# Three small loads ahead of the first one, tiles moved by 64 bytes, and the matmuls around two transposes split one and three, in a fused matmul, GELU, matmul

## The chip, the cores and the metric

The kernel runs on one core of one Trainium2 chip. The metric is device time in microseconds (us) of one execution. Five executions of the kernel before took 120.43, 120.38, 120.18, 120.31 and 118.75 us, with a median of 120.31. A profile is one execution recorded by the hardware profiler, and it names the engines PE (matrix engine, with its weight loads as PEld), DVE (vector), ACT (scalar), POOL (GpSimd) and SP (which only issues transfers here).

## What is computed

```python
h = a @ b                                  # a 1024x1024, b 1024x2048, float32
h = 0.5*h*(1 + tanh(sqrt(2/pi)*(h + 0.044715*h**3)))
out = h @ c                                # c 2048x1024
```

The tanh form of GELU is one ACT function. The kernel works with bf16 operands and with sums and differences of them in a 32-bit format.

## The kernel before

**The whole.** The first product is computed transposed, 128 of its 2048 columns at a time, for two halves (0 and 1) of 512 rows of `a`. GELU writes the result to `hT[h]`, which the second product uses as its stationary operand. The first 4 column tiles are made by plain matmuls (`block`, `mm1`). The other 12 and the second product go through `seven`, a scheme that forms the four blocks of a 2x2 block product from seven block products (`zero`, `one` and `two`). There DVE and ACT make the sums (`Seven.dve`, `plain_s`, `plain_t`) and PE accumulates in PSUM.

**The order is written by hand.** Every engine executes its instructions in the order in which the function states them. Waits between engines follow from the tiles that the instructions share.

**Loads.** SP issues twelve loads of 512 KB: eight of `a` into the two `sta` tiles (`load_a(h, q)`: half h, a quarter q of the columns, in runs of 1024 bytes), and four of the first 512 columns of `b` into `stb` (`load_b`, in runs of 2048 bytes). The last load of `a` releases a one-column copy on POOL (`gate`, L82), and behind it POOL issues the other loads of `b` and those of `c`, with a cast to bf16 on the way (L87 to L93). ACT issues no load. Its first instruction is a GELU on one column (L83), ahead of which its function table is loaded.

**The opening.** PE first multiplies zeros (`stir`, four pieces on `warm`) while the first load is under way. `cast_a` then casts a quarter of `a` to bf16 (`ab`), on DVE, on ACT or half on each. `turn(h, q, i, ab)` transposes it in two steps, n = 0 and n = 1, of four PE transposes each. Both steps write the same PSUM tile `pt`, and after each of them DVE copies 128x512 elements from it to `aT` (L131). `next(tn)` runs one step. Between the two steps of a turn stand some matmuls of the step before. For the turns of half 1 these are the last two tiles of a `block` of four (the first two stand ahead of the turn). For half 0 they are a block of three.

```python
block(0, range(2), (3,))
tn = turn(1, 1, 7, ab)
next(tn)
block(0, range(2, 4), (3,))
next(tn)
```

The opening is followed by `seven(zero)`, `seven(one)` and `seven(two)`, nearly all of whose PE work is L195.

**Tiles.** `consts` is a pool of small tiles. The pools `keep`, `big` and `small` come behind it in memory, so its length moves every other tile. The first of them, `c_sb`, starts at byte 17,856 of its partition, which is 34 times 512 plus 448. All later tiles have lengths that are multiples of 512, and so have the same remainder. The tag `o` is a ring of four tiles of 128x512 for results (`plus`, and the copies in `done2`), from which the stores are made.

**Stores.** `done2(i, l, j, p)` stores a block of 128x512 of the result through SP. Blocks with (i, l) = (0, 0) are stored in two halves of 256 columns. The last two pieces of the kernel are made from a ring of their own (`e`, L377 to L379).

Of the kernel before, what the change touches and what calls it, by code (L numbers as in the profile page):

```python
# [9 lines left out]
F32 = mybir.dt.float32  # L10
# [9 lines left out]
def kernel(ctx, tc, a, b, c, out):  # L20
    nc = tc.nc
# [3 lines left out]
    H = 512  # L25
# [8 lines left out]
    consts = ctx.enter_context(tc.tile_pool(name="consts", bufs=1))  # L34
# [11 lines left out]
    def pieces(tag, bufs, shape, dt, name):  # L46
        return small.tile(shape, dt, name=name, tag=tag, bufs=bufs)
# [5 lines left out]
    gate = consts.tile([128, 1], F32, name="gate")  # L53
    g = consts.tile([128, 1], F32, name="g")

    c_sb = keep.tile([128, NT, P], BF16, name="c_sb")
    hT = [keep.tile([128, NT, H], BF16, name=f"hT{h}") for h in range(2)]
    aT = slot("a", [128, 2, KT, H], BF16, "aT")
# [8 lines left out]
    def load_a(h, q):  # L67
        nc.sync.dma_start(out=sta[q // 2][:, h, q % 2],
                          in_=av[:, 4 * h:4 * h + 4, ds(q * 256, 256)])

    def load_b(q):
        nc.sync.dma_start(out=stb[:, 2 * q:2 * q + 2], in_=bv[:, 2 * q:2 * q + 2, 0:H])

    load_a(0, 0)
    load_b(0)
    load_a(1, 0)
    for q in range(1, 4):
        load_a(0, q)
        load_b(q)
        load_a(1, q)  # L80
# [7 lines left out]
    for n in range(2):  # L88
        for k in range(0, KT, 4):
            nc.gpsimd.dma_start(out=b2[:, k:k + 4, ts(n, H)],  # L90
                                in_=bv[:, k:k + 4, ds(1024 + n * H, H)])
# [9 lines left out]
    def mm1(p, t, h, ks):  # L101
        for k in ks:
            nc.tensor.matmul(p, b1[:, k, ts(t, 128)], aT[:, h, k],  # L103
                             start=(k == 0), stop=(k == KT - 1))
# [20 lines left out]
    def turn(h, q, i, ab):  # L125

        pt = bank(i, (128, 2, H), BF16, "pt")
        for n in range(2):
            for m in range(4):
                nc.tensor.transpose(pt[:, n, ts(m, 128)], ab[:, m, ts(n, 128)], ident)  # L130
            nc.vector.tensor_copy(aT[:, h, 2 * q + n], pt[:, n])  # L131
            yield
# [6 lines left out]
    def block(h, tiles, ks):  # L139
        for k in ks:  # L140
            for t in tiles:
                mm1(ps[h, t], t, h, (k,))
# [93 lines left out]
    cast_b(3)  # L236
    ab = cast_a(1, 1, nc.vector, nc.scalar)
    block(0, range(4), (2,))
    block(0, range(2), (3,))
    tn = turn(1, 1, 7, ab)  # L240
    next(tn)
    block(0, range(2, 4), (3,))
    next(tn)
    zero.t1(4, 1)
    ab = cast_a(0, 2, nc.scalar, nc.scalar)
# [6 lines left out]
    cast_b(5)  # L252
    ab = cast_a(1, 2, nc.vector, nc.scalar)
    block(0, range(4), (4,))
    block(0, range(2), (5,))
    tn = turn(1, 2, 7, ab)
    next(tn)
    block(0, range(2, 4), (5,))
    next(tn)
    zero.t1(4, 2)  # L260
    ab = cast_a(0, 3, nc.scalar, nc.scalar)
# [169 lines left out]
    def store(mt, q0, w, ot, eng=None):  # L431
        (eng or nc.sync).dma_start(out=out[ts(mt, 128), ds(q0, w)], in_=ot)

    def done2(i, l, j, p):
        if (i, l) == (1, 0):
            ot = pieces("o", 4, [128, H], F32, "ot")
            nc.vector.tensor_copy(ot, p)
            p = ot
        n = 2 if (i, l) == (0, 0) else 1
        for q in range(n):  # L440
            r = ds(q * (H // n), H // n)
            store(4 * i + j, l * H + q * (H // n), H // n, p[:, r])

    def between2(n):
        if n == "P1":
# [11 lines left out]
        elif n == "P73":  # L457
            two.t4(two.t[1], 4)

    seven(two, done2, between2)  # L460


# [28 lines left out]
```

## Time and profile before

| What | Value |
|---|---|
| Median of five executions | 120.31 us (118.75 to 120.43) |
| The profiled execution: its own time | 120.43 us |
| Its span, first to last instruction | 118.7 us |
| PE busy | 113.4 us, 96% of the span |
| DVE, ACT, POOL busy | 90.5, 59.3 and 11.0 us |
| First load, from its issue until what waits for it can go on | 0.74 to 4.28 us |
| Opening (turns and plain matmuls) on PE | 5.05 to about 27.2 us |
| The three `seven` stages on PE | about 27.2 to 115.4 us |
| SP's loads | 512 KB each, 9 us in the middle from issue to landing |

The profiled time is 1.7 us above the span; this lies around the program's instructions. A busy PE means that some matmul is in the pipeline. Whether it runs at its full rate is seen only from how far the starts of two matmuls lie apart.

### The profile page before, as it was taken

Reading aid. Unit: us, or ns where it says so; the run is one execution under the profiler, and the core shown is the slowest. Engines: PE = TensorE matmul, PEld = TensorE weight load, DVE = VectorE, ACT = ScalarE, POOL = GpSimd, SP = SyncE. Lnnn points to the kernel's source line nnn. Section 1 sums busy time; section 2 is a strip of 40 time slices with the busy share of each in tenths; the row PEclk is TensorE's granted clock in tenths of the full one; section 3 lists DMA queues with packets and bytes.
Section 4 is the critical chain, followed back from the end, with each engine's and each line's share of the span. In section 5 each row is a group of like instructions: output and inputs, shape, how many; then the busy total and the mean of one; then the engine's idle time right before and its main releaser. Section 6 shows DMA issues by size and latency. Waiting matters only on the chain.

```text
span 118.7 us, 1478 instructions
## 1 busy us (share of the span) xinstructions
PE 113.4 (96%) x540; PEld 77.8 (66%) x540; DVE 90.5 (76%) x107; ACT 59.3 (50%) x99; POOL 11.0 (9%) x21
## 2 busy tenths in 40 slices
PE   5899999999999999999999999999999999999990
PEld 5464554554777545888887444488888888888860
DVE  0331666889999799971779999999999986964570
ACT  5066577489648989446769446900042992000000
POOL 2000029722332000000000000000000000000000
PEclk9999999999999999999999999999999999999999
DMA  2999999999999999997000000061000002004993
GB/s 87 281 372 364 365 355 336 207 207 206 206 208 211 211 211 213 212 210 147 3 0 0 0 6 0 0 200 65 0 0 0 0 0 94 0 29 175 363 355 139
DMA packets 13542, 17.91 MB, mean 151 GB/s; under 512 B 736, under 2 KB 8928, under 8 KB 13536
## 3 DMA queue, kind: packets, MB, share of 16 engines
q0 software_dynamic: 5344, 7.34, 34.8%
q1 hardware_dynamic: 8192, 10.49, 26.0%
q8 instruction: 4, 0.07, 0.2%
q14 instruction: 2, 0.02, 0.0%
HBM read 20.97 MB, written 4.19 MB: 212 GB/s over the span
## 4 chain that ended last, share of the span: by engine, by line
PE 91%; DMA 3%; DVE 2%; issue 0%
PE ps L195 74%; PE ps L103 12%; PE pt L130 4%; DMA sta<-in_a_dram 3%; DVE aT L131 1%; PE ps L114 1%; DVE ab L99 1%; DVE ot L378 0%
## 5 line engine op out<-in xcount | busy, mean ns | idle before, releaser
L195 PE MATMUL ps<-x,s 128*128 128x512 f32 x128 | 29.6, 391 | 0.0
L195 PEld LDWEIGHTS ps<-x,s 128*128 128x128 f32 x128 | 24.0, 188 | 5.1
L195 PE MATMUL ps<-x,x 128*128 128x512 f32 x96 | 22.9, 394 | 0.0
L195 PEld LDWEIGHTS ps<-x,x 128*128 128x128 f32 x96 | 18.0, 188 | 3.9
L103 PE MATMUL ps<-aT,b 128*128 128x512 bf16 x64 | 17.5, 402 | 0.0
L301 ACT ACTIVATE v<-ps 128x512 f32<-128x512 f32 x10 | 6.0, 598 | 19.4 <-PE ps L195 19.4
L195 PE MATMUL ps<-c_sb,hT 128*128 128x512 bf16 (+1 forms) x72 | 14.2, 356 | 0.0
L195 PE MATMUL ps<-x 128*128 128x512 f32 x56 | 13.2, 393 | 0.0
L131 DVE COPY aT<-pt 128x512 bf16<-128x512 bf16 x16 | 6.8, 423 | 8.2 <-PE pt L130 8.2
L195 PEld LDWEIGHTS ps<-x 128*128 128x128 f32 x56 | 10.2, 188 | 2.7 <-ACT u L301 0.4
L195 PEld LDWEIGHTS <-hT 128*128 128x128 bf16 x72 | 6.9, 98 | 7.0 <-issue 0.5
L107 ACT ACTIVATE hT<-ot 128x512 bf16<-128x512 f32 x18 | 10.6, 627 | 1.6 <-DVE ot L306 1.4
L306 DVE TENSOR_TENSOR ot<-ps,u 128x512 f32<-128x512 f32 x10 | 6.8, 690 | 5.4 <-ACT u L301 5.4
L306 DVE TENSOR_TENSOR ot<-ps,v 128x512 f32<-128x512 f32 x10 | 6.7, 688 | 5.3 <-DMA out_dram<-ot 3.9
L195 PE MATMUL ps<-aT,b 128*128 128x512 bf16 x48 | 10.7, 379 | 0.0
L153 DVE TENSOR_TENSOR x<-c_sb 128x1024 fp32r<-128x1024 bf16 x8 | 9.2, 1217 | 0.0
L130 PEld LDWEIGHTS <-ab 128*128 128x128 bf16 x64 | 5.0, 102 | 6.3 <-issue 3.4
L103 PEld LDWEIGHTS <-b 128*128 128x128 bf16 x64 | 6.0, 103 | 4.7 <-issue 1.1
L195 PEld LDWEIGHTS <-b 128*128 128x128 bf16 x48 | 4.6, 98 | 5.7 <-issue 0.3
L107 ACT ACTIVATE hT<-ps 128x512 bf16<-128x512 f32 x14 | 7.3, 597 | 1.6 <-PE ps L103 1.6
L97 ACT ACTIVATE ab<-sta 128x512 bf16<-128x512 f32 x10 | 6.0, 625 | 4.2 <-DMA sta<-in_a_dram 3.4
L301 ACT ACTIVATE u<-ps 128x512 f32<-128x512 f32 x10 | 5.9, 597 | 3.4 <-PE ps L195 3.2
(39 smaller groups left out, 116.2 us busy)
## 6 DMA issues: line engine op xcount, KB each, us to landing
sta<-in_a_dram SPq DMA_DIRECT2D x8, 512.0 KB, 9.1
c_sb<-in_c_dram POOLq DMA_DIRECT2D x8, 512.0 KB, 19.8
b<-in_b_dram POOLq DMA_DIRECT2D x6, 512.0 KB, 11.8
out_dram<-ot SPq DMA_DIRECT2D x12, 256.0 KB, 2.1
stb<-in_b_dram SPq DMA_DIRECT2D x4, 512.0 KB, 8.7
out_dram<-ot SPq DMA_DIRECT2D x8, 128.0 KB, 2.0
```

The source lines that it names most:

```text
L97: nc.scalar.activation(dst, src, AF.Copy)
L99: nc.vector.tensor_copy(dst, src)
L103: nc.tensor.matmul(p, b1[:, k, ts(t, 128)], aT[:, h, k], start=(k == 0), stop=(k == KT - 1))
L107: nc.scalar.activation(hT[h][:, t], p, AF.Gelu_apprx_tanh)
L114: nc.tensor.matmul(ps[0, 3][:, 0:w], warm[:, 0:128], warm[:, 0:w], start=True, stop=True, skip_group_check=True)
L130: nc.tensor.transpose(pt[:, n, ts(m, 128)], ab[:, m, ts(n, 128)], ident)
L131: nc.vector.tensor_copy(aT[:, h, 2 * q + n], pt[:, n])
L153: nc.vector.tensor_tensor(out=dst[:, r], in0=x[:, r], in1=y[:, r], op=op)
L195: nc.tensor.matmul(p[:, ds(c0, w)], l[:, k, ts(j, 128)], r[:, k, ds(c0, w)], start=(start and k == 0), stop=(k == self.kt - 1), skip_group ...
L301: nc.scalar.activation(st, p, AF.Copy)
L306: nc.vector.tensor_tensor(out=ot, in0=p, in1=st, op=ADD)
```

## The change

Four things are changed.

1. `consts` gets one more tile of 64 bytes for each partition, `room`, that nothing uses. All tiles of the pools behind it move by 64 bytes, `c_sb` to 17,920, which is 35 times 512.
2. Ahead of SP's loads three small loads are issued from ACT: 12, 8 and 4 rows of `b`, 2048 bytes each, to as many partitions (from 96, 64 and 32 on) of a tile `lag`, which nothing reads. The loads are spread over 12, 8 and 4 of the 16 DMA engines. `lag` is the first tile taken from the ring `o`, so all later ones move on by one place.
3. In turns (1, 1) and (1, 2) one matmul of the block stands ahead of the turn and three between its two steps, in place of two and two.
4. `done2` stores the blocks with (i, l) = (0, 0) whole, as all others: three stores of 256 KB in place of six of 128 KB.

```diff
     g = consts.tile([128, 1], F32, name="g")
 
+    consts.tile([128, 16], F32, name="room")
+
     c_sb = keep.tile([128, NT, P], BF16, name="c_sb")
...
+    lag = pieces("o", 4, [128, H], F32, "lag")
+    for n in (12, 8, 4):
+        nc.scalar.dma_start(out=lag[8 * n:9 * n], in_=b[0:n, 0:H])
 
     load_a(0, 0)
...
     block(0, range(4), (2,))
-    block(0, range(2), (3,))
+    block(0, range(1), (3,))
     tn = turn(1, 1, 7, ab)
     next(tn)
-    block(0, range(2, 4), (3,))
+    block(0, range(1, 4), (3,))
     next(tn)
...
-    block(0, range(2), (5,))
+    block(0, range(1), (5,))
     tn = turn(1, 2, 7, ab)
     next(tn)
-    block(0, range(2, 4), (5,))
+    block(0, range(1, 4), (5,))
     next(tn)
...
-        n = 2 if (i, l) == (0, 0) else 1
-        for q in range(n):
-            r = ds(q * (H // n), H // n)
-            store(4 * i + j, l * H + q * (H // n), H // n, p[:, r])
+        store(4 * i + j, l * H, H, p)
```

## The prediction

> **What bounds the kernel now.** I read the page first, for which engine sets the end:
>
> ```profile
> span 118.7 us, 1478 instructions
> ...
> PE 113.4 (96%) x540; PEld 77.8 (66%) x540; DVE 90.5 (76%) x107; ACT 59.3 (50%) x99; POOL 11.0 (9%) x21
> ...
> PE 91%; DMA 3%; DVE 2%; issue 0%
> ```
>
> PE carries the chain that ended last; transfers are in it for 3% (the first load), DVE for 2%. From 27.4 to 115.4 us the chain is one piece, L195, 400 matmuls in 88.0 us. At the 0.216 us that lie between two starts of 512 columns in the trace, and half of it for the 16 short ones, these need 84.7 us. Nothing of the change touches this stretch but the place of its operands. What can be won lies ahead of it, so I read the chain in order of time (start, length, what):
>
> ```profile
> 0.74 3.54 DMA sta<-in_a_dram
> ...
> 8.15 2.52 PE ps L103 x6
> ...
> 13.62 1.29 PE ps L103 x6
> 14.91 0.24 PE pt L130 x4
> 15.15 0.02 issue
> 15.18 0.44 DVE aT L131
> 15.61 0.04 issue
> 15.65 0.38 PE pt L130 x4
> 16.04 0.65 PE ps L103 x3
> 16.68 0.25 PE pt L130 x4
> 16.94 0.65 PE ps L103 x3
> 17.59 0.29 PE pt L130 x4
> ```
>
> Three things are to be seen. The first load starts everything. The first six plain matmuls take 0.42 us each and later ones 0.215: PE ran at half its clock until 10.49 us, where the trace's only record of a granted full clock begins (the page's clock row shows full speed in the first slices only because no record covers them). And in turn (1, 1) the chain leaves PE for DVE's copy between the two steps (15.15 to 15.65), while in turn (0, 2), with three matmuls between its steps, it stays on PE.
>
> Last, the timeline, for what the first step of a turn waits for (start, length, engine, line, idle time before and its releaser):
>
> ```profile
> 14.00 0.42 DVE L99 CAST ab<-sta 128x512 bf16<-128x512 f32 x1
> ...
> 18.25 0.70 DVE L99 CAST ab<-sta 128x512 bf16<-128x512 f32 x1
> ...
> 19.01 0.23 PEld L130 LDWEIGHTS <-ab 128*128 128x128 bf16 x4 [0.34 <-DVE ab L99]
> ```
>
> The casts of turns (1, 1) and (1, 2) are the same work; the second takes 0.70 us, while POOL is issuing its loads (17.08 to 23.0 us), and PE's weight loads wait for it.
>
> **One and three.** The starts of PE's matmuls give the hole: in turn (1, 1) the second matmul between the steps starts at 15.191 and the first transpose of step 1 at 15.654, 0.463 us later where 0.216 is due: 0.247 lost. In turn (0, 2), with three between, it is 0.248, so 0.032 lost. A third matmul fills the hole: 0.247 - 0.032 = 0.215 us, one matmul. It is won only if step 0 can start one matmul earlier. In turn (1, 1) DVE's cast ends at 14.42, a weight load follows such an end by 0.06 (18.95 to 19.01), so step 0 can start at 14.48; with five matmuls instead of six behind the transposes of turn (0, 1) it is due at 14.54. It fits by 0.06 us: 0.215 won. In turn (1, 2) the cast ends at 18.95, and step 0 starts at 19.01 already, 0.01 late. One matmul earlier it would be due at 18.79 and would stall 0.22 us for the cast: the hole moves from behind step 0 to ahead of it, and nothing is won. That the cast shrinks to 0.42 (then 0.215 more) needs it to miss POOL's issuing. POOL's gate opens when the last load of `a` has landed (16.93), and the cast stays inside the 6 us of issuing even if that is 1.7 us sooner. Bounds 0 and 0.215; I take 0, by the row of this very cast. What is late next is the copy's end again, by 0.03 us.
>
> **64 bytes.** The packets of SP's loads last 46 ns for 1024 bytes and 84 to 88 ns for 2048 (the trace's packets; middle values). [...] The first load is 512 packets, 32 for each DMA engine: 32 x 4 ns = 0.13 us sooner (bounds 0 and 0.26).
>
> Over the whole of SP's loads (1.8 to 20.7 us, about 350 GB/s) 8% is 1.5 us, but this is hidden: the transposes of turn (0, 3) start at 20.83 and ACT's cast for them ends at 19.63, over 1 us earlier, and no PE wait in this profile is for a load behind the first. Should PE come earlier by more than that, the loads would bind. The last store, 128 runs of 1024 bytes, 8 for each DMA engine, gains 8 x 4 ns = 0.03 us on the tail.
>
> **Three small loads.** ACT has no DMA issue in this profile, so the cost is bounded. On ACT: SP's issues take 0.33 us (128 packets) to 0.42 (512), so three take 1.0 to 1.3 us. They push the table load (0.73 to 2.01) and the column behind it (2.03) to an end near 3.6 us; ACT's next work is at 6.64, after an idle of 4.41. Hidden with 3 us to spare. On the DMA engines: 3, 2, 1 and 0 packets of 84 ns on four engines each, 0.25 us at most, if they go ahead of the first load. [...] No trace here shows an ACT queue. If issuing too is shared, SP's first issue could stand behind one small issue, 0.33 us, or all three, 1.0. Below nothing: the small loads could take the slow first packets (200 to 280 ns on some engines near 2.1 us) off the first load, up to 0.2 us. So the first load lands between 0.2 sooner and 1.25 later; I take 0.25 later, by the packet row, and with the 0.13 above 0.1 later.
>
> This delay does not cost its full length: if the clock is released at 10.49 whatever PE's start, a shift of 0.1 us moves 0.1 us of half-rate work behind the release, where it takes half. Cost 0.05 us (bounds -0.2 and +0.5).
>
> **Ring and stores.** The ring `o` only changes the numbers of its tiles. Three issues fewer on SP at 77 to 80 us; no PE wait is for them, and SP idles 17.7 us behind. Where they matter is the release of an `o` tile for DVE 15 us later. 0.
>
> **The sum.** -0.215 + 0.05 - 0.03 = -0.2 us of the profiled 120.43, which is 120.2. The profiled execution stands 0.12 above the median; from 120.31 the same step gives 120.1. That is 0.2%, well within the 1% that a measurement of this kernel can tell from no change.
>
> **The rivals.** *The clock decides (chance 0.27).* The fifth execution, 118.75, is 1.7 us below the profiled one. [...] Then PE meets the loads, the 8% count too, 0.2 to 0.5 us: 118.75 - 0.2 - 0.3 = 118.3, between 118.0 and 118.6. [...]
>
> *A window later (0.08), the slower side.* [...]
>
> *No effect of the two turns (within the forecast's chance).* The cast of turn (1, 1) runs into POOL's issues too, if the gate opens before 14.0; 120.3.
>
> **How the numbers follow.** Forecast 0.65: between 119.7 (both turns, no delay) and 120.7 (no turn, 0.5 of delay). Early clock 0.27, late clock 0.08. The range from 118.1 to 120.9 leaves out the late clock and a tail on either side. Faster by over 1% (below 119.1): 0.27; slower by over 1% (above 121.5): 0.08; within: 0.65.
>
> **What would show it.** In the profile of the changed kernel the chain stays on PE through turn (1, 1), with 0.25 us ahead of its second step; turn (1, 2) keeps a hole of 0.2 us ahead of its first step, behind a cast of 0.70. Packets of 1024 bytes take 42 ns (46 would say that 64 bytes are nothing), and POOL's gate opens 1 us or more before 16.93. The first cast starts at about 4.4 instead of 4.30, and the first plain matmuls lie 0.43 apart until 10.5. What makes me wrong is the release of the clock at another window, or a first load later by 1 us.

## The result, and the profile after

| | before | changed |
|---|---|---|
| median of all executions | 119.01 us (76) | 118.30 us (39) |
| lowest, highest | 118.60, 120.76 | 118.09, 120.41 |
| executions below 119.65: number, median | 50, 118.94 | 25, 118.24 |
| executions above it: number, median | 26, 120.37 | 14, 120.13 |
| the profiled execution: its own time, span | 120.43, 118.7 | 120.17, 118.4 |

The ratio is 0.9921, with a 95% interval of 0.9901 to 0.9941. It leaves out executions more than 1.5% above the fastest of their kernel, which is all 14 of the changed kernel's upper group but only a part of before's, so that I also compare like with like: 118.24 against 118.94 is 0.994, and 120.13 against 120.37 is 0.998. The changed kernel is faster by 0.7 us where both are in the lower group and by 0.2 where both are in the upper one, less than 1%.

Both kernels have two groups of executions, and here nothing between them. The traces tell which is which: in profiles of the lower group TensorE's full clock is granted between 4.2 and 6.8 us after the start of the span, in those of the upper group between 9.97 and 10.60. I call them early and late clock. (Until then matmuls start 0.43 us apart instead of 0.215.) Four of the five times that the forecast started from were late; of 76 only 26 are. The changed kernel has the same share of late ones beside it, 36% against 34%. The share itself wanders: in the groups of runs below, 31 to 55% of the executions of the kernel before are late.

The profiled execution of the changed kernel is a late one too, as that of before is, and so the two can be compared line by line. The page of the changed kernel:

```profile
span 118.4 us, 1478 instructions
...
PE 112.7 (95%) x540; PEld 77.7 (66%) x540; DVE 90.5 (76%) x107; ACT 59.2 (50%) x99; POOL 11.5 (10%) x21
...
PE 91%; DMA 3%; DVE 2%; issue 1%
```

PE is busy for 0.7 us less, and the chain has the same shares. The chain of waits that ended last in the changed kernel, in order of time (start, length, what):

```profile
0.74 4.10 DMA sta<-in_a_dram
...
8.71 1.98 PE ps L110 x6
...
13.64 1.08 PE ps L110 x5
14.72 0.22 PE pt L137 x4
14.95 0.65 PE ps L110 x3
15.60 0.25 PE pt L137 x4
...
18.06 0.71 DVE ab L106
18.77 0.05 issue
18.82 0.40 PE pt L137 x4
19.21 0.65 PE ps L110 x3
...
27.19 87.99 PE ps L202 x400
```

The first load takes 4.10 us in place of 3.54. In turn (1, 1) (14.72 to 15.85) the chain now stays on PE, with five matmuls ahead and three between the steps. In turn (1, 2) it leaves PE ahead of the first step, for a cast of 0.7 us (18.06). The last piece is as long as before (87.99 against 88.0) and starts 0.20 earlier. This sum closes for the two profiles. The third matmul in turn (1, 1) takes a hole of 0.247 us to 0.032, which gains 0.215. The delay of 0.56 falls into half-rate work and costs 0.28. The clock comes at 9.97 here and at 10.49 in before's profile, which gives back half of 0.52, or 0.26. Together that is -0.2. The last of the three terms stands in no sum of the forecast, and whether the change or chance brings the clock sooner here, one late profile of the changed kernel can't show.

The timeline of the changed kernel around the casts of turns (1, 1) and (1, 2) (start, length, engine, line, idle time before and its releaser):

```profile
14.02 0.42 DVE L106 CAST ab<-sta 128x512 bf16<-128x512 f32 x1
...
16.28 0.67 POOL L89 COPY gate<-sta 128x1 f32<-128x1 f32 x1 [14.97 <-DMA sta<-in_a_dram]
...
16.89 1.62 POOL L94 DMA_DIRECT2D b<-in_b_dram  x2
...
18.06 0.70 DVE L106 CAST ab<-sta 128x512 bf16<-128x512 f32 x1
...
18.81 0.23 PEld L137 LDWEIGHTS <-ab 128*128 128x128 bf16 x4 [0.55 <-DVE ab L106]
```

POOL's gate opens at 16.28, 0.65 sooner than the 16.93 of before, and the cast at 18.06 lies within one of POOL's issues (17.76 to 18.51 by the trace's single records). In nine of the traces a cast of this shape starts 0.26 to 0.30 us into one of POOL's issues, and each of the nine ends 0.25 us after the end of that issue: for example, issue ends of 18.70, 18.51, 21.78 and 23.08 go with cast ends of 18.95, 18.76, 22.03 and 23.33. Not every overlap does this. Casts that start up to 0.14 us into an issue, or 0.6 us or more into one, take 0.42 to 0.43 us. Why it is so isn't shown.

What the early clock makes of the change isn't seen in this profile. It is the subject of the experiments.

### The profile page after: what moved, and what is told of

It reads as the page before. It is cut to its first block, busy times and chain, and to the rows that moved or that the text cites. A ratio compares the mean times of both kernels' runs of the same rounds, so it can differ in the third digit from the quotient of the medians.

```text
span 118.4 us, 1478 instructions
## 1 busy us (share of the span) xinstructions
PE 112.7 (95%) x540; PEld 77.7 (66%) x540; DVE 90.5 (76%) x107; ACT 59.2 (50%) x99; POOL 11.5 (10%) x21
## 2 busy tenths in 40 slices
DMA packets 13158, 17.96 MB, mean 152 GB/s; under 512 B 712, under 2 KB 8136, under 8 KB 13152
## 3 DMA queue, kind: packets, MB, share of 16 engines
q1 hardware_dynamic: 7760, 10.49, 24.4%
## 4 chain that ended last, share of the span: by engine, by line
PE 91%; DMA 3%; DVE 2%; issue 1%
PE ps L202 74%; PE ps L110 11%; PE pt L137 4%; DMA sta<-in_a_dram 3%; DVE ab L106 1%; PE ps L121 1%; DVE aT L138 1%; DVE ot L385 0%
## 5 line engine op out<-in xcount | busy, mean ns | idle before, releaser
L110 PE MATMUL ps<-aT,b 128*128 128x512 bf16 x64 | 17.0, 393 | 0.0
L308 ACT ACTIVATE v<-ps 128x512 f32<-128x512 f32 x10 | 6.0, 599 | 19.4 <-PE ps L202 19.4
L202 PE MATMUL ps<-aT,b 128*128 128x512 bf16 x48 | 10.7, 379 | 0.0
L137 PE MATMUL pt<-ident,ab 128*128 128x128 bf16 x64 | 6.6, 229 | 1.3 <-DVE ab L106 0.6
```

Of the source, the lines that this page charges most:

```text
L110: nc.tensor.matmul(p, b1[:, k, ts(t, 128)], aT[:, h, k], start=(k == 0), stop=(k == KT - 1))
L202: nc.tensor.matmul(p[:, ds(c0, w)], l[:, k, ts(j, 128)], r[:, k, ds(c0, w)], start=(start and k == 0), stop=(k == self.kt - 1), skip_group ...
L308: nc.scalar.activation(st, p, AF.Copy)
```

## The experiments

Line numbers are those of each kernel. "Early" and "late" medians are those of the two groups above, and ratios are to executions of the kernel before that were measured beside the run. The forecast had it that the change gains one turn's 0.215 us and nothing else. Two theories stand against that. Theory L says that the 64 bytes make the loads faster, and that with an early clock the loads set PE's pace. Theory S says that it is the small loads that do this.

**Each part alone, and the change without its small loads.**

```diff
+    consts.tile([128, 16], F32, name="room")         # e1: only this
```

> The kernel before plus the unused 64-byte tile alone. Theory L (in the execution with the early clock PE waits for SP's loads, and the 64 bytes take the spread of 46 to 58 ns off the load packets): packets of 1024 bytes all 46 ns, POOL's gate 1 us or more sooner, time 0.3 to 0.6 us below before. Rival S (it is the three small loads that put the DMA engines out of step): packets keep their spread, time within 0.1 us of before.

Median 119.07 us; early 118.86, late 120.38, against 118.92 and 120.4 of before; ratio 0.9976 (0.9939 to 1.0014). How the loads run between 6.5 and 16 us is read from the stretch's table: length, then busy time of PE, PEld, DVE, ACT and POOL, the clock, the share of the DMA engines and GB/s. First before, then the changed kernel, then this one:

```profile
6.50:16.00 9.50, 9.33 (x54) 5.10 (x52) 3.82 (x9) 6.55 (x13) 0.00 (x0) 1.00 1.08 365
```

```profile
6.50:16.00 9.50, 9.18 (x56) 5.38 (x56) 4.12 (x11) 7.06 (x13) 0.00 (x0) 1.00 1.08 390
```

```profile
6.50:16.00 9.50, 9.13 (x64) 4.75 (x64) 5.22 (x12) 6.96 (x13) 0.00 (x0) 1.00 1.07 386
```

The 64 bytes alone bring the loads from 365 to 386 GB/s, and yet almost no time. The clock isn't what makes the rate: in the profiles with an early clock of e13 (tiles as in before) and e14 (the whole change) it is 363 and 390. The packets show where the rate comes from. In before, over the same stretch, 97% of those of 1024 bytes last from 46 to 58 ns and 97% of those of 2048 from 84 to 100; here nearly all last 46 and 84. The shortest packet stays as it was, and the longer ones are gone. So theory S is out, and theory L is right about the packets but not about the time.

```diff
+    lag = pieces("o", 4, [128, H], F32, "lag")       # e2: only this
+    for n in (12, 8, 4):
+        nc.scalar.dma_start(out=lag[8 * n:9 * n], in_=b[0:n, 0:H])
```

> The kernel before plus the three small loads alone. Theory L: the first cast starts about 0.5 us later (4.8 instead of 4.30), packets keep their spread, time 0.2 to 0.5 us above before. Rival S: the spread goes, time 0.3 to 0.6 us below before.

Median 119.56; early 119.34, 0.42 above before; ratio 1.0038 (1.0 to 1.0077). The packets keep their spread, and the loads run at 360 GB/s. Of the cost, 0.32 us lies at the kernel's very end: from the last start on PE to the end of the span it takes 3.85 us, and 3.53 in before. SP's waits there (us in all, times, longest) are, in this kernel and then in before:

```profile
SPq L491 <- DMA out_dram<-ot: 1.4, 3, 0.6
```

```profile
SPq L486 <- DMA out_dram<-ot: 1.1, 2, 0.6
```

SP checks its outstanding transfers one after another at the end, in an order that goes with their numbers. Each check of one that has landed takes about 0.06 us (0.059 to 0.069 from start to start in before). Which one is checked where has changed: here the store that lands last is the fourth of nine checks, so that five others follow it, about 0.3 us; in before it is the last.

```diff
-    block(0, range(2), (3,))                         # e3: only this, for
+    block(0, range(1), (3,))                         # (3,) and for (5,)
...
-    block(0, range(2, 4), (3,))
+    block(0, range(1, 4), (3,))
```

> The kernel before with one and three matmuls about turns (1, 1) and (1, 2) alone. If PE sets the pace there: 0.2 us below before, from turn (1, 1) alone, with the hole of turn (1, 2) moved ahead of its first step. If with the early clock the loads set the pace there: within 0.1 us of before.

Late 119.88, against 120.4: 0.5 gained, and the profile (a late one, 119.85) has holes of 0.03 us in both turns. The cast of turn (1, 2) isn't held, though POOL is issuing:

```profile
17.23 1.62 POOL L87 DMA_DIRECT2D b<-in_b_dram  x2
...
17.96 0.42 DVE L99 CAST ab<-sta 128x512 bf16<-128x512 f32 x1
```

It starts 0.73 us into the first issue (17.23 to 18.10), where the changed kernel's starts 0.30 us into the second. So with a late clock turn (1, 2) is won or lost by where the cast falls among the issues. Early 118.93, against 118.92: nothing gained, though on four executions only (e17 below has sixteen). So the turns are worth up to two matmuls with a late clock and nothing with an early one, which no theory said.

```diff
-    lag = pieces("o", 4, [128, H], F32, "lag")       # e4: changed kernel
-    for n in (12, 8, 4):                             # without these
-        nc.scalar.dma_start(out=lag[8 * n:9 * n], in_=b[0:n, 0:H])
```

> The changed kernel without its three small loads (64 bytes, turns and whole stores stay). Theory L: the first load lands 0.4 to 0.5 us sooner than in the changed kernel, time 0.2 to 0.5 us below it, near 117.9. Rival S: time above the changed kernel by 0.3 to 0.6 us, near 118.7.

Median 118.46; early 118.37 (19 of 22), ratio 0.9908 (0.9873 to 0.9942). The gain is there without the small loads, and so are the faster loads, 388 GB/s.

**The same kernels again.** The kernel before (e5; its profile is late, 120.67), the changed kernel (e6), and the changed kernel without the 64 bytes (e7).

```diff
-    consts.tile([128, 16], F32, name="room")         # e7: changed kernel without this
```

> The kernel before unchanged, for a profile of an execution with the early clock. The clock's release stands near 5 to 7 us instead of 10.49, the span is about 117.2, and PE has waits for casts behind loads in the opening that the profile with the late clock doesn't show: theory L says that they add up to 0.4 us or more. Rival: hardly any, and the opening is set by PE and DVE with the early clock too.

> The changed kernel, on the same chip as the next ones. About 118.25, 0.7 us below the kernel before where the clock comes early, 0.25 below where it comes late; the two holes of the turns and the waits for loads are gone together.

> The changed kernel without the 64-byte tile (small loads, turns and whole stores stay). If turns and 64 bytes pay only together: 119.2 to 119.4, the 0.4 us of the small loads above before. If the turns pay by themselves: 118.9 to 119.1, and without the small loads it would be below before.

The changed kernel: 118.38, early 118.26 and late 120.16, ratio 0.9909 (0.987 to 0.9948). Its profile is early (118.07), and its timeline has the answer to the late one above:

```profile
12.19 0.43 DVE L106 CAST ab<-sta 128x512 bf16<-128x512 f32 x1
12.67 0.23 PEld L137 LDWEIGHTS <-ab 128*128 128x128 bf16 x4 [0.37 <-DVE ab L106]
...
16.28 0.43 DVE L106 CAST ab<-sta 128x512 bf16<-128x512 f32 x1
...
16.76 0.23 PEld L137 LDWEIGHTS <-ab 128*128 128x128 bf16 x4 [0.38 <-DVE ab L106]
```

PE comes 1.9 to 2.1 us earlier than in the late profile, so the cast of turn (1, 2) is ahead of POOL's issuing, which begins at 16.33, and lasts 0.43 us. Neither of these casts waits for a load. PE loses 0.04 and 0.05 us ahead of the two first steps: both turns are won.

Without the 64 bytes: early 119.05, ratio 1.0009 (0.9972 to 1.0045). All of the gain is gone. The two casts now start as their loads land, and PE loses 0.292 and 0.325 us ahead of the first steps:

```profile
12.79 0.43 DVE L104 CAST ab<-sta 128x512 bf16<-128x512 f32 x1 [0.30 <-DMA sta<-in_a_dram]
...
17.18 0.43 DVE L104 CAST ab<-sta 128x512 bf16<-128x512 f32 x1 [0.32 <-DMA sta<-in_a_dram]
```

So in the early clock the turns are won only if the 64 bytes are there.

**Is it the clock?** Theory C, as the expectations call it, has it that PE's idle time in the opening makes the clock late, and that every execution is early without it. To have the clock early at each execution, three more pieces on zeros were put where PE is idle in the opening, in before (e8), in the changed kernel (e10) and in it without the small loads (e11).

```diff
-    stir(256, 256, 256, 256)
-    for _ in turn(0, 0, 4, cast_a(0, 0, nc.vector)):
-        pass
+    stir(256, 256, 256, 256, 64)
+    tn = turn(0, 0, 4, cast_a(0, 0, nc.vector))
+    next(tn)
+    stir(128, 64)
+    next(tn)
     stir(256, 128)
```

> The kernel before with three more pieces of multiplied zeros (64 columns ahead of the first transposes, 128 and 64 between their two steps), so that PE has no idle of 0.3 and 0.7 us there. [...] Rival (the slow executions have another cause, such as the loads): about a third stay near 120.4.

> The kernel before unchanged, once more for a profile of an execution with the early clock. If the loads set the pace there: the first steps of turns (1, 1) and (1, 2) start 0.4 us behind casts that themselves start at about 12.7 and 17.05, as their loads land, and the last load of a comes late or not. If PE and DVE set it: the casts start when the turn ahead is done, not when the load lands.

> The changed kernel with the three pieces of multiplied zeros of e8. Theory C with the 64 bytes in place: no execution near 120.1, the last load isn't late as in e8, all between 118.1 and 118.7; median 0.5% below before in its faster executions. Rival: the last load comes 1 us late as in e8, 119.3 to 119.6.

> The changed kernel without the small loads and with the three pieces of e8. All executions between 118.1 and 118.7 if the small loads are worth nothing in the changed kernel; 0.1 to 0.2 above e10 if they bring the loads of a in sooner, as two profiles with and two without them hint (POOL's gate at 16.21 and 16.28 with them, 16.38 and 16.40 without).

> The kernel before with an unused tile of 320 bytes in place of 64, which puts all later tiles at 256 past a multiple of 512. If the rule is of 256 bytes: packets all 46 and 84 ns, as in e1, and POOL's gate near 16.4. If it is of 512: packets spread to 58 ns and the gate near 16.95, as before.

The kernel before (e9) has a late profile again; of its ten executions five are early and five late, with a median of 119.58. The other three have their releases at 5.55, 4.22 and 5.90 us and lie in one group each but for two executions of e10, and yet they are slow: 119.95, 118.95 and 119.02. Ratios 1.0056 (1.0029 to 1.0082), 0.9967 (0.9937 to 0.9998) and 0.9986 (0.9963 to 1.0009). The expectation of an early group that is simply larger failed. What came instead is seen in ACT's timeline: e8, then e11.

```profile
22.55 0.63 ACT L97 ACTIVATE ab<-sta 128x512 bf16<-128x512 f32 x1 [1.61 <-DMA sta<-in_a_dram]
```

```profile
21.66 0.63 ACT L100 ACTIVATE ab<-sta 128x512 bf16<-128x512 f32 x1 [1.67 <-DMA sta<-in_a_dram]
```

ACT waits 1.6 us for the last load of `a`; PE then waits for ACT, 1.07 us in e8, 0.73 in e10 and 0.87 in e11. A load reports its end in sixteen parts (in before's trace, 512 packets of 4 bytes for SP's 32 transfers). In e11 fifteen of them have come by 20.24 and the sixteenth at 21.55; in e10 it is 20.48 and 21.69, in e8 21.20 and 22.45. Just before that the traces have a packet of the program's own instructions, 16 KB, which takes 0.96 to 1.16 us from 19.4 to 20.1 us on. That this packet holds the DMA engine of the late part is argued from the times, as the trace doesn't name the engine. So these three kernels carry a second disturbance, and understate what an early clock is worth. Why the other profiles, which have such a packet too, show no part so late stays open.

```diff
+    consts.tile([128, 80], F32, name="room")         # e12: before, 320 bytes
```

The tiles of e12 start 256 bytes past a multiple of 512. Median 118.85, early 118.83 (16 of 20), ratio 0.9967 (0.9931 to 1.0002); nearly all packets at 46 and 84 ns, 387 GB/s between 6.5 and 16 us. So at 256 past a multiple of 512 the packets are as even as at a multiple itself (e1), and only at before's 448 are they spread.

**The same, with no instruction added.** The two pieces behind the turn are cut in another way, so that one of them stands between its steps: in before (e13), in the changed kernel (e14), and in before with single parts of the change.

```diff
-    for _ in turn(0, 0, 4, cast_a(0, 0, nc.vector)):
-        pass
-    stir(256, 128)
+    tn = turn(0, 0, 4, cast_a(0, 0, nc.vector))
+    next(tn)
+    stir(192)
+    next(tn)
+    stir(192)
```

> The kernel before with its last two pieces of zeros (256 and 128 columns, behind the first turn) made 192 and 192, the first of them between the two steps of that turn, where PE idles 0.7 us; no instruction more. Theory C: no execution near 120.4, all near 118.9; the last load of a isn't late by 1 us. The casts of turns (1, 1) and (1, 2) start near 12.7 and 17.05, as their loads land, and the first steps 0.4 us behind. Rival (the late executions have another cause): a third stay near 120.4.

> The changed kernel with the pieces moved in the same way. Theory C: no execution near 120.1, all between 118.1 and 118.5, so a median of about 118.3 and a mean 0.7 below the changed kernel's.

> The kernel before unchanged. With the clock early: casts of turns (1, 1) and (1, 2) near 12.7 and 17.05 when their loads land, first steps near 13.2 and 17.5. With it late: as e5 and e9, near 14.9 and 19.1.

> e13 (the kernel before with the six pieces of zeros moved, 118.91) plus the 64-byte tile. If the loads alone set the pace: 118.6. If, as the profile of e1 shows, the 0.3 us that the loads bring are given back at turn (1, 3), where DVE's cast is held up while POOL issues a load: 118.8 to 118.9.

> e13 plus the two turns. If the casts behind the loads hold the first steps (starts near 13.1 and 17.5 as in e13): 118.7 to 118.9, at most 0.2 won at the holes behind them. If the turns pay fully without the 64 bytes: 118.5.

> e13 plus 64 bytes, turns and whole stores, so e14 without the small loads. 118.2 to 118.3 if the small loads are worth nothing in the changed kernel, 118.35 to 118.4 if they bring 0.1 to 0.2.

(e18 has the 64 bytes, the turns and the whole stores, without the small loads. e15, before as it is, came out late once more, 120.49.)

All 22 executions of e13 (118.75 to 119.24) and all 14 of e14 (118.06 to 118.65) are in the early group, where before, measured beside them, had 11 late ones among 35. e13's median is 118.91, ratio 0.9975 (0.9954 to 0.9996); e14's is 118.22, ratio 0.9917 (0.9888 to 0.9945). By the mean of all executions, which counts the late ones, e14 takes 118.26 us; in the comparison at the top the changed kernel takes 118.94, and before 119.42. e14 is the best version of the study.

e13 shows before with an early clock, which none of before's own profiles has. In before PE waits between the two steps of the first turn:

```profile
6.18 0.58 PE L130 MATMUL pt<-ident,ab 128*128 128x128 bf16 x4 [0.52 <-DVE aT L131]
```

The timeline of e13, with the opening and then the two casts:

```profile
5.22 0.61 PE L130 MATMUL pt<-ident,ab 128*128 128x128 bf16 x4 [0.24 <-DVE ab L99]
...
5.62 0.63 PE L114 MATMUL ps<-warm 128*128 128x192 f32 x2
...
6.34 0.38 PE L130 MATMUL pt<-ident,ab 128*128 128x128 bf16 x4
...
12.63 0.43 DVE L99 CAST ab<-sta 128x512 bf16<-128x512 f32 x1 [0.43 <-DMA sta<-in_a_dram]
...
17.02 0.43 DVE L99 CAST ab<-sta 128x512 bf16<-128x512 f32 x1 [0.32 <-DMA sta<-in_a_dram]
```

The piece at 5.62 fills the 0.52 us. Both casts wait for a load that has just landed: in the early clock the loads, not PE, set the pace of turns (1, 1) and (1, 2). They cost PE 0.055 and 0.10 us ahead of the first steps, and the holes of 0.247 behind these steps are there as in the late clock.

e17, the turns alone on top of that:

```profile
13.08 0.43 DVE L99 CAST ab<-sta 128x512 bf16<-128x512 f32 x1 [0.41 <-DMA sta<-in_a_dram]
...
17.45 0.43 DVE L99 CAST ab<-sta 128x512 bf16<-128x512 f32 x1 [0.29 <-DMA sta<-in_a_dram]
```

The casts still wait for the loads, and step 0, due one matmul earlier, waits 0.292 and 0.311 us. That is the hole of before, moved to the front. This profile is the slowest of e17's sixteen executions (119.33), with loads 0.4 us later than in e13; but e7, a typical one, has the same two waits.

e16, the 64 bytes alone on top, at turn (1, 3):

```profile
20.92 1.46 POOL L95 DMA_DIRECT2D c_sb<-in_c_dram  x2
...
21.20 0.72 DVE L101 CAST ab<-sta 128x512 bf16<-128x512 f32 x1
...
21.84 1.21 DVE L155 TENSOR_TENSOR x<-aT,x 128x1024 fp32r<-128x1024 bf16 x1
...
22.97 0.41 DVE L133 COPY aT<-pt 128x512 bf16<-128x512 bf16 x1
...
23.43 0.38 PE L132 MATMUL pt<-ident,ab 128*128 128x128 bf16 x4 [0.18 <-DVE aT L133]
```

PE reaches the first step of this turn at 22.21, 0.43 ahead of e13. But DVE's cast at 21.20 falls into one of POOL's issues and takes 0.72, the sum behind it comes later, and so does the copy that PE waits for. The second step starts at 23.43, only 0.12 ahead of e13's 23.55.

e18, the two together, at the same place:

```profile
20.89 0.42 DVE L102 CAST ab<-sta 128x512 bf16<-128x512 f32 x1
21.22 1.22 DVE L156 TENSOR_TENSOR x<-aT,x 128x1024 fp32r<-128x1024 bf16 x1
22.36 0.42 DVE L134 COPY aT<-pt 128x512 bf16<-128x512 bf16 x1
```

Everything has come forward by another 0.3 us. The cast starts together with POOL's issue (20.89 too) and isn't held. PE's second step is at 22.83.

The early clock's sum is now closed but for e17. Columns: the second step of turn (1, 3), the time from PE's last start to the end, the sum of both differences against e13, and the medians' difference.

| kernel | second step (1, 3) | tail | sum | median, difference measured |
|---|---|---|---|---|
| e13, before with pieces moved | 23.55 | 3.54 | | 118.91 |
| e16, with 64 bytes | 23.43 | (not used) | -0.12 | 118.80, -0.11 |
| e17, with the turns | (slow profile) | (not used) | (not formed) | 118.90, -0.01 |
| e18, both, and whole stores | 22.83 | 3.68 | -0.58 | 118.34, -0.57 |
| e14, the whole change | 22.89 | 3.49 | -0.71 | 118.22, -0.69 |

The two parts give -0.11 and -0.01 alone, and -0.57 together. Their ratios against before (0.9897, 0.9931 and 0.9861, each with about 0.005 on either side) hold little, as 12 of the 22 executions of before beside them are late; so the medians of these kernels are compared, all measured on one chip. Medians of 5 (e16) and 6 executions (e18, with one at 120.56, unexplained) are thin, but the traces carry the same sums.

What e14 gains on e13 can be read from the starts of the matmuls. The two holes give 0.43 us (0.247 to 0.031 in each turn). Waits for loads, from turn (0, 1) to turn (1, 2), give 0.35: 0.086 to 0.030, 0.188 to nothing, 0.055 to 0.024 and 0.100 to 0.028. e14 starts turn (1, 0) 0.13 later. That is 0.65 of the 0.67 us by which its second step of turn (1, 3) is ahead.

## Why the prediction was right or wrong

The time, 118.30, lies within the range of 118.1 to 120.9, and the change is within 1%, as the likeliest case had it. The predicted 120.1 was too high, and the gain of 0.2 too small for two executions in three. The steps that failed are two terms that the sum put at nothing: the faster loads ("this is hidden") and turn (1, 2) ("I take 0"). With an early clock the loads' waits are worth 0.35 us (of which a later start takes back 0.13) and turn (1, 2) another 0.22 (e13 to e14), so that the median falls by 0.7. Both terms were read from one profile with a late clock, taken as the typical execution; that also put the start at 120.31, where the median of 76 is 119.01.

**The premise.** The profile and the median of five were taken as the typical execution; both were late ones, and the early group is the larger. For the late group the number agrees, -0.2 said and -0.24 measured, but in part by luck: in the late profile the delay costs 0.28 instead of 0.05, and a clock that comes 0.52 us sooner, which the sum didn't have, pays for it. The rival "the clock decides" gave 118.3, made of the fifth execution's 118.75, -0.2 for a turn and -0.3 for the loads. Its time is what came, and it is that of the early group. But the change doesn't make more executions early: 36% are late, against 34% of before. That PE's idle time in the opening decides between early and late is shown by e13 and e14 (36 of 36 early, with nothing added); of e16 to e18, 26 of 27 are early. It is the wait between the two steps that counts here: ahead of the first step PE still idles 0.67 us in e14. The full clock's record lasts 109.226 us in every late profile and 112.640 in every early one but e4's (109.226), which is 3.414 us more. At half rate 3.414 us cost 1.7, by estimate; late minus early is 1.4 us in before and 1.9 in the changed kernel, on either side of that. What sets these lengths isn't shown.

**One and three.** "I take 0" for turn (1, 2) was right for the profile at hand: the hole moved ahead of step 0, to 0.222 us, behind a cast of 0.70. It is not so for every late clock: in e3 the cast stays inside the issuing, as the forecast had it, and yet takes 0.42. And it was wrong in the early clock, where that cast is ahead of POOL's issuing and both turns are won, up to 0.43 us. The bound of 0.215 was stated; the reason for taking the other end failed. There is also an error in what I took POOL's gate to wait for, here and in the description of the kernel: it isn't the last load of `a` but that of its third quarter for half 1, the ninth of twelve loads.

**64 bytes.** This is the step that failed, twice. The 4 ns that the forecast takes off each packet of 1024 bytes (46 to 42), and with them its 0.13 and 0.03 us, its 8% and the bound of 0.26, are shown by no run: the packets stay at 46. What goes is the spread above it, which I had in the same trace and left out by using middle values: the rate rises by 7%, near the 8% forecast, from another place in the distribution. The gate came 0.65 sooner, not 1. The second failure weighs more: "this is hidden: ... over 1 us earlier" was derived in the late clock alone. PE is 1.5 to 2 us ahead in the early one, and the loads bind. The condition ("should PE come earlier by more than that, the loads would bind") stood beside it and should have been carried into the forecast. But faster loads alone gave 0.1 (e1, e16), since the lead was lost again at turn (1, 3); only with the turns does it hold.

**Three small loads.** Predicted 0.1 us on the first load's landing; measured 0.56 on the first cast of the two late profiles (4.30 to 4.86), so this term was mis-sized. Part of that is scatter: over all profiles the first cast starts at 4.14 to 4.71 us without the small loads and at 4.57 to 5.02 with them. Most packets of the small loads take 81 to 116 ns, near the 84 assumed, but four of the 24 take 608 to 780 (in e2, twelve take 552 to 1181). It was nearly harmless, as the release of the clock takes half of it in the late group, and in the early group the loads ahead of turn (1, 1) set the pace anyway. It is within the bounds given, up to 1.25.

**Ring and stores.** "0" holds in the body. At the end it doesn't: small loads alone make the tail 0.32 us longer, and with the rest of the change they make it 0.18 shorter (3.69 without, 3.51 with). The order of SP's checks accounts for both: in e4, without them, the last store to land is the sixth of nine checks, and three more checks of 0.06 us follow. That is read from the traces and not tested by itself; whole stores were never run alone.

**A window later.** The slower side did not come: the first cast started 0.56 us later, and yet the full clock came at 9.97 in the late profile, against 10.49 in before's. The highest of 39 executions is 120.41, and slower by over 1% began at 121.5.

## What to carry to other kernels

Before a forecast rests on a profile, look at where its execution stands among all times: with two groups, the profile tells of one, and each wait called hidden has to be worked out again for the other. Two edits of which each alone is worth next to nothing can be worth much together when a wait only moves between two neighbours (here a load and a copy), so a bound taken with one part fixed is no bound on both. And PE's idle time in the opening may decide when the clock comes: moving work that is there already to fill it did better here (e13, e14) than adding work (e8, e10).

## What was not expected of the hardware

- Tiles that start at 448 past a multiple of 512 bytes don't make the shortest packet longer (46 ns either way for 1024 bytes); they spread the packets to 58 ns (2048 bytes: 84 to 100). At a multiple of 512 (e1) and at 256 past one (e12) nearly all last 46 and 84.
- One of a load's sixteen parts can come 1.2 to 1.3 us after the others (e8, e10, e11), behind what is probably a packet of the program's own instructions (16 KB, 0.96 to 1.16 us).
- DVE's cast of 128x512 takes 0.42 us, and 0.70 to 0.76 when it starts 0.26 to 0.30 us into one of POOL's DMA issues: it then ends 0.25 us after the issue. One that starts together with the issue (e18, at 20.89) or 0.73 us into it (e3, at 17.96) isn't held.
- At the kernel's end the order in which finished transfers are checked is worth up to 0.3 us.
